# Hybrid attention layer on one core: transfers pinned behind weight pieces, and the query group's parts redistributed

## The chip, the cores and the metric

One NeuronCore of a Trainium2 chip runs the whole kernel. The metric is device time in microseconds (us) of one execution. Engines: PE (TensorE matmul), PEld (its weight load), DVE (VectorE), ACT (ScalarE), POOL (GpSimd) and SP (SyncE, which here only issues transfers).

## The reference

One encoder layer on 1024 tokens of width 2048, all float32:

```
u = rmsnorm(h); z = u @ w_in                    # 2048 x 9216
q, k, v, gate (16 heads x 64), and an HGRN2 group of 8 heads x 128
q = rope(q) / 8;  k = rope(k)
res = [band_attention(q, k, v, w, d) for (w, d) in ((128,1), (512,4), (2048,16))]
o_att = softmax over the three log denominators, weighted sum;  y_att = o_att * silu(gate)
y_hg  = rmsnorm(forward scan + backward scan) * silu(its gate)
h = h + rmsnorm([y_att, y_hg] @ w_out)
h = h + rmsnorm(sigmoid(h @ w_pg) * (p @ w_pp))
```

The change touches the attention heads alone: the products q, k and gate, the banded softmax, and the product with v.

## The kernel before, in words

The stages follow each other: normalise x and project all v (0 to about 400 us), eight HGRN2 heads (to about 1290 us), eight pairs of attention heads (to about 2100 us), then the output projection and the two gates. Every product with a weight matrix is made three times over (high x high, low x high, high x low), so a weight piece of 512 x 128 (256 KB) costs a load on SP, a cast `wh` on ACT (L83), a subtraction `wl` on POOL (L84), a cast `wb` on DVE (L85) and, for both halves of the tokens, 16 matmuls with `wh` and `wl` (L102, L103) and 8 with `wb` (L107). `raw`, `wh`, `wl` and `wb` have three buffers each, so loads run three pieces ahead of PE.

A group (q, k or gate of one pair) is four pieces. `group_parts` is a generator: after the matmuls of a piece that end half 0 of the tokens it yields (16 high and 4 low matmuls: an odd part), and after the 4 low ones of half 1 it yields again (an even part). Eight parts make a group; one more step calls `sink`, which evacuates both halves. A group takes two of the four `gb` banks of PSUM, and there are three kinds of groups in flight, so a group begins when an earlier one's banks have been evacuated. The four other banks (`wk`) serve scores, transposes and values.

`Pair` is a pair of heads:

- `queries()` and `keys()` evacuate through `rope_evac`: `araw` on ACT (L521), an exchange of rows by small transfers into `apart` (L525, L526), `apr` on POOL (L528), `araw` times cosine on DVE (L529), then the sum, `aq` (L576) or `akn` (L557). A key half is then split into `akh` (L560) and `akn` (L561) and copied by four transfers into the key tiles `ak` (L565, L566).
- `q_half(hf)` splits the query half `aq` on ACT (`aqh`, L589) and DVE (L590) and copies it by eight transfers of 128 KB into `aqt` (L594), which has one buffer.
- `loads()` brings V in two arrangements, `avc` (L602, two transfers of 256 KB) and `avn` (L609, four of 64 KB and four of 192 KB), one buffer each.
- `scores(hf, fill)`: eight units of score matmuls `asc` (L637), each reduced and masked on DVE (L646) and exponentiated on ACT (L649), then a softmax exchange: per-query minima and sums are moved between partitions (`aoth`, L657) and turned into factors `afm` (L661 to L670). After every second unit it takes one part from `fill`.
- `values(hf, fill)`: eight turns scale the probabilities (`asm`, L690 on ACT, L692 on DVE), transpose them on PE (`apt`, L694), copy them (`aPT`, L697) and multiply with V (`ao`, L706 with `avn`, L709 with `avc`); then `ayt` (L719). It takes a part of `fill` at the second and the sixth turn.
- `gate()` evacuates with a sigmoid (`sg`, L728), two products (L729, L730) and a store to `yD` (L731).

The evacuations share the tag `h2` with five buffers: `araw`, `apr`, `akn`, `akh`, `aq`, `aqh` and `sg`.

Order: a scheduler orders each engine's instructions ahead of time, by the order in which the program traces them and by when it takes them to be ready; weight pieces (load and casts) are given a priority 3000 places ahead. [...] `keep_in_program_order` fixes an instruction behind the one traced last on its engine, and `after(x, mark)` issues x behind mark; neither adds a wait for a result.

The loop over pairs, before, with a the pair and b the next:

```
a.loads(); g = a.gate(); a.scores(0, g)            # 4 gate parts
run(bq, 4); a.q_half(1); a.values(0, bq); a.scores(1, bq); run(bq)
run(g, 2); run(b.keys(), 9); b.q_half(0); a.values(1, islice(g, 2)); run(g)
```

Of the kernel before, what the change touches and what calls it, by code (L numbers as in the profile page):

```python
# [12 lines left out]
F32 = mybir.dt.float32  # L13
# [9 lines left out]
S = 1024  # L23
# [14 lines left out]
def f32(t):  # L38
    return t.bitcast(F32)
# [6 lines left out]
class Kern:  # L46
    def __init__(self, tc, ctx):
        self.tc = tc
        self.nc = tc.nc
        self.ctx = ctx  # L50
        nc = self.nc
        self.cp = ctx.enter_context(tc.tile_pool(name="cp", bufs=1))
        self.wp = ctx.enter_context(tc.tile_pool(name="wp", bufs=3))
        self.ps = ctx.enter_context(tc.tile_pool(name="ps", bufs=1, space=PSUM))
        self.dr = ctx.enter_context(tc.tile_pool(name="dr", bufs=1, space=DRAM))
        self.ident = self.cp.tile([128, 128], F32, name="ident")
        make_identity(nc, self.ident)
        self.rest = None
# [481 lines left out]
    class Pair:  # L540
        def __init__(self, K, w_in, hp, vsrc, yout):
            self.K, self.w_in, self.hp, self.vsrc, self.yout = K, w_in, hp, vsrc, yout
            self.nat = (slice(0, 64), slice(64, 128))
            self.qn = {}
            self.sm = {}
            self.fac = {}

        def keys(self):
            K, nat = self.K, self.nat
# [32 lines left out]
        def q_half(self, hf):  # L582
            K, nat = self.K, self.nat
            nc = K.nc
            V = nc.vector
            q = self.qn.pop(hf)
            self.QT = [K.big.tile([128, 2, 512], F32R, name=f"aqt{i}", tag=t, bufs=1) for i, t in enumerate(("hv", "O"))]
            qh = K.h2("aqh")
            nc.scalar.copy(qh.bitcast(F32R), q)  # L589
            V.tensor_tensor(q.bitcast(F32R), q, qh, op=ALU.subtract)  # L590
            for sq, src in ((0, qh), (1, q)):
                for h in range(2):
                    for o in range(2):
                        nc.sync.dma_start(f32(self.QT[sq])[nat[o], h], src[nat[h]])  # L594

        def loads(self):
            K, vsrc = self.K, self.vsrc
            nc = K.nc
            self.vn = K.big.tile([128, 8, 2, 128], F32, name="avn", tag="ht", bufs=1)
            self.vc = K.big.tile([128, 4, 2, 128], F32, name="avc", tag="hvt", bufs=1)  # L600
            for k in range(2):
                nc.sync.dma_start(self.vc[:, :, k], vsrc[512 * k:512 * k + 512, :].rearrange("(p r) e -> p r e", r=4))  # L602
            row = vsrc.ap[0][0]
            for i0, st, n in ((0, 7, 2), (1, 1, 6)):
                t0 = K.wstart(i0)
                step = (K.wstart(i0 + st) - t0) * row
                for r in range(4):
                    src = bass.AP(tensor=vsrc.tensor, offset=vsrc.offset + (t0 + r) * row, ap=[[4 * row, 64], [step, n], [1, 128]])
                    nc.sync.dma_start(self.vn[64 * (r % 2):64 * (r % 2) + 64, i0:i0 + st * (n - 1) + 1:st, r // 2], src)  # L609
            self.yt = K.big.tile([128, S], F32, name="ayt", tag="gt", bufs=1)  # L610

        def scores(self, hf, fill):
            K, KS, QT = self.K, self.KS, self.QT
# [57 lines left out]
            self.sm[hf] = sm  # L671
            self.fac[hf] = m

        def values(self, hf, fill):
            K, vn, vc, yt = self.K, self.vn, self.vc, self.yt
            nc = K.nc
            V = nc.vector
            sm, f = self.sm.pop(hf), self.fac.pop(hf)
            o = K.wk("ao")
            ov = o.rearrange("p (i r b) -> p i r b", i=4, r=4)  # L680
            steps = [(l, i) for i in range(4) for l in range(2)]
            pt = {}

            def turn(n):
                l, i = steps[n]
                p = K.wk("apt", (128, 2, 2, 128))
                for h in range(2):
                    d = sm[h][:, l, i]
                    if h:
                        nc.scalar.activation(d, d, AF.Copy, scale=f[:, l, h, i:i + 1])  # L690
                    else:
                        V.tensor_scalar(d, d, f[:, l, h, i:i + 1], None, op0=ALU.mult)  # L692
                    for c in range(2):
                        nc.tensor.transpose(p[:, h, c], d[:, 128 * c:128 * c + 128], K.ident)  # L694
                if n % 2 == 0:
                    pt[n // 2] = K.big.tile([128, 2, 2, 2, 128], F32, name="aPT", tag=("KD", "hq")[n // 2 % 2], bufs=1)
                (nc.scalar.copy if n % 2 else V.tensor_copy)(pt[n // 2][:, n % 2], p)  # L697

            def use(n):
                l, i = steps[n]  # L700
                P = pt[n // 2][:, n % 2]
                for c in range(2):
                    for h in range(2):
                        hs = slice(64 * h, 64 * h + 64)
                        if l:
                            nc.tensor.matmul(o[hs, 128 * i:128 * i + 128], vn[:, 4 * hf + i, c, hs], P[:, h, c],  # L706
                                             start=False, stop=(n == 7 and c == 1), skip_group_check=True)
                        else:
                            nc.tensor.matmul(ov[hs, :, i, :], vc[:, i, c, hs], P[:, h, c].rearrange("p (i b) -> p i b", i=4),  # L709
                                             start=(n == 0 and c == 0), stop=False, skip_group_check=True)  # L710

            for n in range(10):
                if n < 8:
                    turn(n)
                if n in (1, 5):
                    next(fill, None)
                if n >= 2:
                    use(n - 2)
            nc.scalar.copy(yt[:, 512 * hf:512 * hf + 512].rearrange("p (i b r) -> p i r b", i=4, r=4), ov)  # L719

        def gate(self):
            K = self.K
            nc = K.nc

            def sink(hf, p):
                sl = slice(512 * hf, 512 * hf + 512)
                sg = K.h2("sg")
                nc.scalar.activation(sg, p, AF.Sigmoid)  # L728
                nc.vector.tensor_tensor(sg, p, sg, op=ALU.mult)  # L729
                nc.gpsimd.tensor_tensor(sg, sg, self.yt[:, sl], op=ALU.mult)  # L730
                nc.sync.dma_start(self.yout[:, sl], sg)  # L731
            return K.group_parts(self.w_in, 3072 + 128 * self.hp, sink)


# [1 line left out]
def tile_hybrid(ctx, tc, x, p, positions, w_in, w_out, g_pre, g_post, g_hg, lb_fwd, lb_bwd, w_pg, w_pp, g_ple, out):  # L736
    nc = tc.nc
    K = Kern(tc, ctx)
# [52 lines left out]
    with tc.tile_pool(name="big", bufs=1) as big:  # L791
        K.big = big
        for h in range(8):
            K.hgrn(w_in, h, vD[2 + h // 4][:, 128 * (h % 4):128 * (h % 4) + 128], yD[8 + h])
            if h == 0:
                with tc.issue_after(late[0].ins), tc.issue_after(late[1].ins):
                    K.att_consts(positions)
        heads = [K.Pair(K, w_in, hp, vD[hp // 4][:, 128 * (hp % 4):128 * (hp % 4) + 128], yD[hp]) for hp in range(8)]

        def run(parts, n=8):  # L800
            for _ in range(n):
                next(parts, None)

        run(heads[0].queries(), 9)
        K.flush()
        run(heads[0].keys(), 9)
        heads[0].q_half(0)
        for n, a in enumerate(heads):
            b = heads[n + 1] if n < 7 else None
            a.loads()  # L810
            g = a.gate()
            if n == 0:
                run(g, 4)
            a.scores(0, g)
            bq = b.queries() if b else iter(())
            run(bq, 4)
            a.q_half(1)
            a.values(0, bq if b else g)
            a.scores(1, bq if b else islice(g, 1))
            run(bq)  # L820
            if b:
                if n:
                    run(g, 2)
                run(b.keys(), 9)
                b.q_half(0)
            a.values(1, islice(g, 1 if n == 7 else 2) if n else iter(()))
            run(g)
    fin = ctx.enter_context(tc.tile_pool(name="fin", bufs=1))
    Y = [fin.tile([128, 4, D], F32, name=f"Y{i}", tag=f"Y{i}") for i in range(2)]
    yss = [fin.tile([128, 4, 4], F32, name=f"yss{i}") for i in range(2)]  # L830
# [255 lines left out]
```

## Time and profile before

| what | us |
|---|---|
| median of 3 runs | 2906.26 (2904.66 to 2910.24) |
| the profiled execution's own time | 2900.24 |
| its span, first to last instruction | 2898.5 |
| PE busy | 2726.5 (94%) |
| attention stage, 1290 to 2100 us | 810, PE busy 745.07 |
| stops of PE at the changes of pair, 1 to 6, and their ends | 9.54 to 1430.44, 4.22 to 1530.27, 4.88 to 1629.62, 4.44 to 1728.71, 5.05 to 1828.22, 5.59 to 1928.10 |
| stops before the first transpose of `values(0)`, pairs 0 to 6 | 1.82, 2.04, 1.78, 1.79, 1.78, 1.79, 1.78 |

A busy time is that of one engine's instructions. A row of the waits gives the waiting engine, line and tile, what released it, then the total in us, how often, and the longest. A row in order of time gives start, duration, engine, line, operation, output and inputs, how many were merged, and in brackets how long the engine had been idle before it and what ended that. A row for a window gives busy time (and number of instructions) of PE, PEld, DVE, ACT and POOL, then the clock granted to PE (1.00 is full), the share of the 16 DMA engines' time, and GB/s. In the rows below, SPq is SP's queue of transfers to issue.

### The profile page before, as it was taken

What the parts mean: (1) busy time and instruction counts of PE and PEld (TensorE: products, weight loads), DVE (VectorE), ACT (ScalarE), POOL (GpSimd) and SP (SyncE); (2) the same over time, 40 slices, a digit from 0 to 9 for tenths busy, and PEclk for the clock granted to TensorE, in tenths of its full rate; (3) what the DMA queues carried; (4) which work ended last, traced back from release to release, by engine and by line L of the source; (5) the groups of instructions that cost most, each with busy time, mean ns of one, the idle gap of its engine ahead of it and who ended that gap; (6) DMA issues with size and microseconds to landing.
All of it is one profiled execution on the core that took longest, in us unless ns stands there. A gap on an engine that the chain in (4) does not pass through costs nothing. (4 is left out here: it accounts for less than half of the span.)

```text
span 2898.5 us, 45014 instructions
## 1 busy us (share of the span) xinstructions
PE 2726.5 (94%) x16853; PEld 1893.5 (65%) x17104; DVE 1449.1 (50%) x3105; ACT 951.3 (33%) x1998; POOL 1047.7 (36%) x833
## 2 busy tenths in 40 slices
PE   6999999999999999999899999989899899999997
PEld 4666666666676666676666666667566566666664
DVE  8601116856356356354555445544755545555545
ACT  5311112222122122123445445544733233333323
POOL 2422223313313313322222232222244554666555
PEclk9999999999999999999999999999999999999998
DMA  6412221211111111123323332342444543444453
GB/s 226 123 55 78 79 84 41 66 49 41 59 49 41 59 49 41 59 59 89 101 59 90 104 97 55 99 108 78 124 139 133 157 146 95 133 113 111 141 155 112
DMA packets 272218, 267.75 MB, mean 92 GB/s; under 512 B 22784, under 2 KB 187648, under 8 KB 270848
## 3 DMA queue, kind: packets, MB, share of 16 engines
q1 hardware_dynamic: 262832, 255.92, 30.7%
q10 hardware_dynamic: 9168, 8.93, 0.9%
q8 instruction: 135, 2.21, 0.3%
q14 instruction: 83, 0.68, 0.1%
HBM read 208.16 MB, written 29.36 MB: 82 GB/s over the span
## 5 line engine op out<-in xcount | busy, mean ns | idle before, releaser
L84 POOL TENSOR_TENSOR wl<-raw,wh 128x512 fp32r<-128x512 f32 x568 | 771.0, 1361 | 1520.7 <-ACT wh L83 1484.0
L85 DVE CAST wb<-raw 128x512 bf16<-128x512 f32 x584 | 406.6, 699 | 817.2 <-PE gb L107 311.8
L83 ACT CAST wh<-raw 128x512 fp32r<-128x512 f32 x584 | 358.1, 617 | 1280.2 <-PE gb L102 474.7
L102 PE MATMUL gb<-uh,wh 128*128 128x512 f32 x1792 | 743.2, 415 | 24.3 <-DMA aqt<-aqh 19.7
L103 PE MATMUL gb<-uh,wl 128*128 128x512 f32 x1792 | 709.5, 396 | 0.0
L107 PE MATMUL gb<-ul,wb 128*128 128x512 bf16 x1635 | 407.6, 380 | 9.0 <-issue 1.3
L102 PEld LDWEIGHTS gb<-uh,wh 128*128 128x128 f32 x1792 | 339.9, 190 | 110.0 <-DVE sg L729 27.0
L103 PEld LDWEIGHTS gb<-uh,wl 128*128 128x128 f32 x1792 | 339.7, 190 | 67.9
L107 PEld LDWEIGHTS <-wb 128*128 128x128 bf16 x1792 | 156.9, 98 | 205.0 <-issue 53.6
L868 PE MATMUL gb<-wh,yh 128*128 128x512 f32 x512 | 231.5, 453 | 7.5 <-DVE Y L900 3.4
L868 PE MATMUL gb<-wh,th 128*128 128x512 f32 x480 | 215.1, 448 | 0.0
L869 PE MATMUL gb<-wl,yh 128*128 128x512 f32 x512 | 203.5, 398 | 5.5 <-POOL wl L84 5.5
L869 PE MATMUL gb<-wl,th 128*128 128x512 f32 x480 | 189.7, 395 | 5.3 <-POOL wl L84 5.3
L872 PE MATMUL gb<-wb,yl 128*128 128x512 bf16 x481 | 136.0, 386 | 1.4 <-issue 0.2
L649 ACT ACTIVATE asm<-asm,aown 128x256 f32<-128x256 f32 x256 | 127.1, 498 | 23.0 <-DVE aown L646 22.5
L872 PE MATMUL gb<-wb,tl 128*128 128x512 bf16 x452 | 126.2, 385 | 1.0
L868 PEld LDWEIGHTS gb<-wh,yh 128*128 128x128 f32 x512 | 97.9, 191 | 37.9 <-issue 3.4
L767 PE MATMUL gb<-wh,uh 128*128 128x512 f32 x256 | 115.4, 457 | 2.0 <-ACT wh L83 2.0
L869 PEld LDWEIGHTS gb<-wl,yh 128*128 128x128 f32 x512 | 97.7, 191 | 25.7 <-POOL wl L84 6.8
L768 PE MATMUL gb<-wl,uh 128*128 128x512 f32 x256 | 101.5, 403 | 10.1 <-POOL wl L84 7.1
L868 PEld LDWEIGHTS gb<-wh,th 128*128 128x128 f32 x480 | 91.0, 190 | 27.5 <-ACT sg L972 2.0
L869 PEld LDWEIGHTS gb<-wl,th 128*128 128x128 f32 x480 | 90.7, 189 | 25.1 <-POOL wl L84 7.6
(284 smaller groups left out, 3646.6 us busy)
## 6 DMA issues: line engine op xcount, KB each, us to landing
raw<-in_w_in_dram SPq DMA_DIRECT2D x320, 256.0 KB
raw<-in_w_out_dram SPq DMA_DIRECT2D x128, 256.0 KB
raw<-in_w_pg_dram SPq DMA_DIRECT2D x128, 256.0 KB
xt<-in_x_dram SPq DMA_DIRECT2D x8, 1024.0 KB
vD<-vo SPq DMA_DIRECT2D x32, 256.0 KB
aqt<-aqh SPq DMA_DIRECT2D x64, 128.0 KB
aqt<-aq SPq DMA_DIRECT2D x64, 128.0 KB
raw<-yD SPq DMA_DIRECT2D x32, 256.0 KB
```

Of the source, the lines that this page charges most:

```text
L83: nc.scalar.copy(wh, raw)
L84: (sub or nc.gpsimd).tensor_tensor(wl, raw, f32(wh), op=ALU.subtract)
L85: nc.vector.tensor_copy(wb, raw)
L102: nc.tensor.matmul(pb[hf], wh[:, k], self.uh[hf][:, kt], start=(kt == 0), stop=False)
L103: nc.tensor.matmul(pb[hf], wl[:, k], self.uh[hf][:, kt], start=False, stop=False)
L107: mm = nc.tensor.matmul(pb[hf], wb[:, k], self.ul[hf][:, kt], start=False, stop=(kt == KT - 1))
L649: nc.scalar.activation(d, d, AF.Exp, scale=-1.0, bias=own[:, 0, loc, h, i:i + 1], accum_out=own[:, 1, loc, h, i:i + 1])
L767: nc.tensor.matmul(pb[t], hi, wh, start=(k == 0), stop=False)
L768: nc.tensor.matmul(pb[t], hi, wl, start=False, stop=False)
L868: nc.tensor.matmul(pb[t], a, pc[0], start=first, stop=False)
L869: nc.tensor.matmul(pb[t], a, pc[1], start=False, stop=False)
L872: nc.tensor.matmul(pb[t], lo[:, k, 128 * t:128 * t + 128], pc[2], start=False, stop=last)
```

## The change

Three things. (1) The transfers of `q_half`, `loads` and the gate's store, which the scheduler placed freely, are each fixed behind what SP had been given before them in the program. `loads()` moves from ahead of the scores to behind the first scores and their gate pieces, and the store of a pair's gated output moves out of the evacuation to the same place in the next pair, ahead of `loads()`. (2) The fills are dealt out anew: five query parts instead of four come before `values(0)`, whose first transpose is issued behind the fifth; `values(0)` and `scores(1)` take one and two; the query evacuation follows `scores(1)`; the first pair keeps two gate parts for `values(1)`; the last pair spreads its gate group over the places where others have queries. (3) `b.q_half(0)` moves from behind the key group to behind its fifth part, and the first transpose of `values(1)` is issued behind the eighth key part.

```diff
@@ Pair.q_half
-                        nc.sync.dma_start(f32(self.QT[sq])[nat[o], h], src[nat[h]])
+                        K.tc.keep_in_program_order(nc.sync.dma_start(f32(self.QT[sq])[nat[o], h], src[nat[h]]))
@@ Pair.loads: both transfers go through this
+            def load(dst, src):
+                K.tc.keep_in_program_order(nc.sync.dma_start(dst, src))
...
-            self.yt = K.big.tile([128, S], F32, name="ayt", tag="gt", bufs=1)
+        def store(self):
+            for sl, sg in self.out:
+                self.K.tc.keep_in_program_order(self.K.nc.sync.dma_start(self.yout[:, sl], sg))
@@ Pair.values
-        def values(self, hf, fill):
+        def values(self, hf, fill, mark):
...
-                        nc.tensor.transpose(p[:, h, c], d[:, 128 * c:128 * c + 128], K.ident)
+                        x = nc.tensor.transpose(p[:, h, c], d[:, 128 * c:128 * c + 128], K.ident)
+                        if n == h == c == 0 and mark is not None:
+                            K.after(x, mark)
@@ Pair.gate
-                nc.sync.dma_start(self.yout[:, sl], sg)
+                self.out.append((sl, sg))
+            self.yt = K.big.tile([128, S], F32, name="ayt", tag="gt", bufs=1)
@@ the loop over pairs
         def run(parts, n=8):
-            for _ in range(n):
-                next(parts, None)
+            return [next(parts, None) for _ in range(n)]
...
-            a.loads()
             g = a.gate()
             if n == 0:
                 run(g, 4)
-            a.scores(0, g)
-            bq = b.queries() if b else iter(())
-            run(bq, 4)
+            bq = b.queries() if b else g
+            a.scores(0, g if 0 < n < 7 else islice(g, 2))
+            if n:
+                heads[n - 1].store()
+            a.loads()
+            marks = run(bq, 5 if b else 3)
             a.q_half(1)
-            a.values(0, bq if b else g)
-            a.scores(1, bq if b else islice(g, 1))
-            run(bq)
+            a.values(0, islice(bq, 1), marks[-1])
+            a.scores(1, islice(bq, 2 if b else 1))
             if b:
+                run(bq)
                 if n:
                     run(g, 2)
-                run(b.keys(), 9)
+                k = b.keys()
+                run(k, 5)
                 b.q_half(0)
-            a.values(1, islice(g, 1 if n == 7 else 2) if n else iter(()))
+                marks = run(k, 4)
+            a.values(1, islice(g, 2 if b else 0), marks[2] if b else None)
             run(g)
+        a.store()
```

More of the change, by code (lines that the diff above doesn't have):

```diff
@@ L546, in __init__ @@
             self.fac = {}
+            self.out = []
         def keys(self):
@@ L601, in loads @@
             for k in range(2):
-                nc.sync.dma_start(self.vc[:, :, k], vsrc[512 * k:512 * k + 512, :].rearrange("(p r) e -> p r e", r=4))
+                load(self.vc[:, :, k], vsrc[512 * k:512 * k + 512, :].rearrange("(p r) e -> p r e", r=4))
             row = vsrc.ap[0][0]
@@ L608, in loads @@
                     src = bass.AP(tensor=vsrc.tensor, offset=vsrc.offset + (t0 + r) * row, ap=[[4 * row, 64], [step, n], [1, 128]])
-                    nc.sync.dma_start(self.vn[64 * (r % 2):64 * (r % 2) + 64, i0:i0 + st * (n - 1) + 1:st, r // 2], src)
-            self.yt = K.big.tile([128, S], F32, name="ayt", tag="gt", bufs=1)
+                    load(self.vn[64 * (r % 2):64 * (r % 2) + 64, i0:i0 + st * (n - 1) + 1:st, r // 2], src)
+        def store(self):
+            for sl, sg in self.out:
+                self.K.tc.keep_in_program_order(self.K.nc.sync.dma_start(self.yout[:, sl], sg))
         def scores(self, hf, fill):
```

## The prediction

> **What bounds the kernel now.** I read the page's busy shares first, then the waits of PE over the attention stage (1290 to 2100 us), then PE, SP and ACT in order of time around one change of head pair.
>
> ```profile
> span 2898.5 us, 45014 instructions
> PE 2726.5 (94%) x16853; PEld 1893.5 (65%) x17104; DVE 1449.1 (50%) x3105; ACT 951.3 (33%) x1998; POOL 1047.7 (36%) x833
> 1290.00:2100.00 810.00, 745.07 (x4299) 535.70 (x4368) 417.96 (x1364) 395.15 (x1012) 226.90 (x213) 0.97 0.34 90
> PE gb L102 <- DMA aqt<-aqh: 19.7, 4, 5.6
> PE apt L694 <- DVE asm L692: 16.3, 10, 2.2
> PE asc L637 <- DMA aqt<-aqh: 9.5, 1, 9.5
> PE gb L102 <- DVE sg L729: 4.4, 1, 4.4
> PE asc L637 <- DMA aqt<-aq: 3.4, 2, 3.1
> ```
>
> PE is the bound: 94% busy, and in attention 745 of 810 us. The third row is a window (PE, PEld, DVE, ACT, POOL busy, clock, DMA share, GB/s). The rest are PE's stops: total, times, longest. Two kinds matter: one long stop per head pair, where PE waits for the transposed query copies (aqt) or for a gate's PSUM bank (sg): 19.7 + 9.5 + 4.4 = 33.6 us over the six changes of pair; and one short stop per pair before the first probability transpose (apt), 16.3 us in all. Attention rows repeat every 99 us, so one change stands for six.
>
> ```profile
> 1524.15 1.90 PE L107 MATMUL gb<-ul,wb 128*128 128x512 bf16 x8
> 1530.27 0.50 PE L102 MATMUL gb<-uh,wh 128*128 128x512 f32 x1 [4.22 <-DMA aqt<-aqh]
> 1513.90 0.70 SPq L525 DMA_DIRECT2D apart<-araw  x1
> 1516.79 1.26 SPq L602 DMA_DIRECT2D avc<-vD  x2
> 1518.14 3.22 SPq L609 DMA_DIRECT2D avn<-vD  x5
> 1522.95 0.63 SPq L565 DMA_DIRECT2D ak<-akh  x1
> 1525.01 0.61 SPq L566 DMA_DIRECT2D ak<-akn  x1
> 1525.72 0.56 SPq L594 DMA_DIRECT2D aqt<-aqh  x1
> 1528.90 2.52 SPq L594 DMA_DIRECT2D aqt<-aq  x4
> 1531.84 1.42 SPq L731 DMA_DIRECT2D yD<-sg  x2
> 1522.73 0.61 ACT L589 CAST aqh<-aq 128x512 fp32r<-128x512 f32 x1
> 1527.60 1.28 ACT L728 ACT_TABLE_LOAD   x1 [2.86 <-DMA ak<-akh]
> 1524.00:1532.00 8.00, 3.78 (x16) 1.95 (x15) 1.86 (x4) 3.60 (x6) 2.91 (x3) 0.94 0.88 233
> ```
>
> PE runs out at 1526.05 and restarts at 1530.27. SP issues one DMA per 0.6 us: seven V loads, then the keys' last four copies, then the eight query copies, until 1531.4; the DMA engines are 88% busy. Two lags end together: the query copies land near 1530.6, and the gate's sigmoid, which must first get an h2 buffer that a key copy still reads (ACT released at 1527.60), frees the bank the next query group needs.
>
> **The change, part by part.** *Query half 0 moves from behind the keys to behind five of their eight parts.* It issues one ACT cast (0.61 us), one DVE subtraction (0.69, row below), eight DMAs (8 x 0.6 = 5 us of SP). They hang behind the third key piece's weight load. In the trace the second q half is summed at 1588.56 to 1590.7, and SP issues nothing but two weight loads from 1591 to 1599.5, so I put the copies there, 25 us before they are needed, and at nothing on PE. If that cover fails, they push the keys' row exchange, issued next at 1599.48, by up to 5 us, and the keys' copies and scores with it.
>
> ```profile
> 1523.46 0.68 DVE L590 TENSOR_TENSOR aq<-aq,aqh 128x512 fp32r<-128x512 f32 x1
> 1588.56 2.18 DVE L576 TENSOR_TENSOR aq<-araw,apr 128x512 f32<-128x512 f32 x1 [2.40 <-POOL apr L528]
> 1591.05 4.15 SPq L76 DMA_DIRECT2D raw<-in_w_in_dram  x2
> 1599.48 0.64 SPq L525 DMA_DIRECT2D apart<-araw  x1
> ```
>
> Late next: the key copies. They still go out at 1522.95 to 1525.6 and, by ACT's release at 1527.60, land about then. PE would wait 1527.60 - 1526.05 = 1.55 us, unless the next query piece runs first; its bank comes free sooner, since two h2 buffers (aq, aqh) are back before the keys' evacuation and the sigmoid need not wait for the key copies. So each stop goes to between 0 (piece first) and 1.55 (scores first). I take the middle, 0.8, as the order on PE is fixed and I can't see it: 33.6 - 6 x 0.8 = 28.8 us saved. Were the copies no earlier at all, nothing would be.
>
> *The clock.* After a long stop PE runs at half clock. Rows: start of a stop's aftermath for pairs 1, 2, 6 (pairs 3 to 5 read 0.79 too), the aftermath of pair 0's 3.1 us stop, and that of the short stop (last):
>
> ```profile
> 1430.00:1438.00 8.00, 7.47 (x31) 6.24 (x32) 3.78 (x12) 3.19 (x7) 4.06 (x5) 0.66 0.71 190
> 1530.00:1538.00 8.00, 7.73 (x36) 6.38 (x37) 3.87 (x14) 2.77 (x5) 3.87 (x6) 0.79 0.79 215
> 1928.00:1936.00 8.00, 7.83 (x30) 6.29 (x30) 2.31 (x8) 1.76 (x5) 3.64 (x5) 0.64 0.79 214
> 1342.00:1350.00 8.00, 7.95 (x35) 6.46 (x36) 0.99 (x4) 1.40 (x4) 0.74 (x2) 0.79 0.27 75
> 1552.00:1560.00 8.00, 6.77 (x62) 4.91 (x64) 5.24 (x13) 5.58 (x13) 0.89 (x2) 1.00 0.01 2
> ```
>
> Lost work is 8 x (1 - clock): 2.7 + 4 x 1.7 + 2.9 = 12.4 us. A 1.78 us stop leaves 1.00, so with stops of 0.8 all 12.4 us come back. If they stay at 3 us, none does. [...]
>
> *Five parts before the first transpose.* The stop after the softmax exchange:
>
> ```profile
> 1550.80 0.59 PE L107 MATMUL gb<-ul,wb 128*128 128x512 bf16 x2
> 1553.18 1.06 PE L694 MATMUL apt<-ident,asm 128*128 128x128 f32 x8 [1.78 <-DVE asm L692]
> 1536.04 0.42 DVE L646 CUSTOM_DVE_ANT_0 asm<-asc,amask 128x256 f32<-128x256 f32 x1 [2.61 <-PE asc L637]
> ```
>
> The fifth part's 16 high matmuls and two of its low ones already run before the stop; the order edge adds only two low ones (0.23 us each), 0.5 us. Two larger shifts come with it: PE reaches this place 1.7 us sooner without half clock, while the scores start sooner against the query piece: now the first reduction comes 1536.04 - 1530.27 = 5.8 us after it, then about 1527.6 + 1.2 (four score matmuls and a query one or two) - 1526.05 = 2.75, 3.0 us better. 1.78 - 0.5 + 1.7 - 3.0 = 0. Ends: 0 and 1.78 + 1.7. Near 0 in the sum, I keep 0.3 per pair: six stops of 1.78 to 2.04 (sum 11.0) become 2, saved 9.
>
> *Stores and V loads.* Twelve DMAs per pair (1.4 us and 10 x 0.63 us of SP) go behind the scores' gate pieces. They then follow the store, issued at 1531.84 already, to about 1540; at 233 GB/s the V tiles' 1.5 MB (2 x 256, 4 x 192 and 4 x 64 KB) and the store's 0.5 MB take 9 us, landed by 1542. First use is after the transposes at 1553: no wait, 10 us of margin. What waits behind them on SP: weight loads, run three pieces (16 us) ahead, and the second query half's copies, now issued at 1538.67 to 1549.9 and used from 1563. Zero; lower end zero too, upper end whatever exceeds 10 us.
>
> *Fills redistributed.* Pair 0 gains two gate parts (5.4 us) in front of the 9.5 us stop, already counted as removed. The same matmuls run. Query evacuation now follows all of the second scores: keys need its banks.
>
> ```profile
> 1563.02 1.21 PE L637 MATMUL asc<-ak,aqt 128*128 128x256 f32 x8
> 1571.85 0.39 PE L102 MATMUL gb<-uh,wh 128*128 128x512 f32 x1
> 1576.72 0.59 ACT L521 ACTIVATE araw<-gb 128x512 f32<-128x512 f32 x1
> 1577.74 0.58 PE L102 MATMUL gb<-uh,wh 128*128 128x512 f32 x1
> 1579.74 0.51 ACT L649 ACTIVATE asm<-asm,aown 128x256 f32<-128x256 f32 x1 [1.40 <-DVE aown L646]
> 1581.69 0.23 ACT L664 ACTIVATE afe<-afe 128x32 f32<-128x32 f32 x1 [1.35 <-DVE afe L663]
> 1583.08 1.31 ACT L690 ACTIVATE asm<-asm,afm 128x256 f32<-128x256 f32 x3 [1.16 <-DVE afm L670]
> ```
>
> Keys start at 1577.74, right behind the evacuation at 1576.72. Behind the last exponential (ends 1580.3) the two evacuations end at 1581.5, against PE work (scores 4.8, query piece 5.6, gate piece 5.4 from 1563.0) that ends at 1578.8: 2.7 us of stop. But that exponential was itself late because rope work took DVE, so the lower end is 0. I take 1.0: +6 over six pairs. Pair 0 keeps its first stop; its short one gives 1. The last pair, with 2 us of stops and thin fills either way, gives 0.
>
> **Sum.** 28.8 + 12.4 + 9 + 1 - 6 = 45 us off the profiled execution's 2900.24 (span 2898.5 and 1.7 around it): 2855. The median of the runs, 2906.26, lies 6.0 (0.2%) above; carried over, 2861.
>
> **Rivals.** *Half the gain*: PE's fixed order puts the scores ahead of the query piece, and the key copies land later than the order was made for, so stops of about 3 us stay. Saved: 33.6 - 18 = 15.6 of the first kind, no clock (by the 3.11 us row), 5 of the short ones, less 6: 15, 2891. [...] For it: every stop now is such a mismatch of order and landing. Against it: 1.55 us is all that the keys' landing leaves.
>
> *The same bytes, no gain*: the boundary is bound by the transfers (88% busy), and the order does not matter: 2906. Against it: 1 MB of query copies (8 x 128 KB) goes to 1591 to 1600, where the engines have room, and the V loads' 1 MB leaves too. [...]
>
> *Slower*: the query evacuation falls on ACT behind the scaling of the second half's probabilities (1583.08 to 1587) and keys wait for the banks: 1588.2 - 1578.8 = 9.4 us and 1.7 of half clock, 11 a pair, 66 over six instead of 6. 2861 + 60 = 2921. It decides for slower once the stop passes some 7 us with its clock 8.5. For it: ACT's order is fixed and there are only four group banks. Against it: the scaling is traced after the keys, the evacuation before.
>
> **How the numbers follow.** Forecast (2840 to 2880) 0.58; half the gain (2880 to 2900) 0.22; no gain 0.06; slower 0.14. A measurement tells about 0.2%, 6 us, from no change: faster 0.80, same 0.06, slower 0.14. The range leaves out the slower case and a little below: both ends of key landing and exchange give 2861 - 5 - 2 - 6 = 2848 at best and 2861 + 5 + 19 + 10 = 2895 at worst, widened to 2842 and to 2905, so that the half-gain case is in.
>
> **What would show it.** Right: the stops on aqt and sg gone or under 1.6 us, clock 1.00 at the change of pair, query copies 25 us ahead of the scores, period near 92 instead of 99 us. Wrong: a new stop in front of keys released by ACT's evacuation (L521), a wait for avc or avn at L709 or L706, or weight casts released by late DMAs (SP blocked behind a pinned copy).

## The result, and the profile after

| | before | changed |
|---|---|---|
| median of the runs, us | 2908.25 (2904.66 to 2910.72, 4 runs) | 2862.28 (2859.64 to 2864.40, 4 runs) |
| profiled execution, us | 2900.24 | 2864.40 |

Changed over before: 0.9842, 95% interval [0.9825, 0.9859], so 1.6% faster, 46 us by the medians. The two profiled executions differ by 36 us only: that of before lies 8 us under its median, that of the changed kernel 2 us above. The traces are therefore read for the places, and the medians for the size.

The changed kernel's page, and PE's waits between the first scores of pair 1 and those of pair 7, first of before, then of after:

```profile
span 2862.6 us, 45162 instructions
PE 2733.1 (95%) x17104; PEld 1891.4 (66%) x17104; DVE 1433.7 (50%) x3105; ACT 949.0 (33%) x1996; POOL 1045.1 (37%) x833
```

```profile
PE gb L102 <- DMA aqt<-aqh: 19.7, 4, 5.6
PE apt L694 <- DVE asm L692: 11.0, 6, 2.0
PE asc L637 <- DMA aqt<-aqh: 9.5, 1, 9.5
PE gb L102 <- DVE sg L729: 4.4, 1, 4.4
PE asc L637 <- issue: 1.2, 1, 1.2
```

```profile
PE asc L645 <- DMA ak<-akn: 22.8, 7, 4.2
```

Five kinds of stop, 45.8 us, have become one, 22.8 us: the scores wait for the key copies. Six of the seven are those at the changes of pair 1 to 6 (19.9 us); the seventh, 2.90 us before the scores of pair 7, stands where before had the 1.2 us of `issue`. (Line numbers have moved down, for the transfers of queries and keys by 1, for the scores by 8, for the gate by 10.) The waits for query copies, for the gate's banks and for the scaled probabilities are gone. The new stop, its surroundings on PE, SP and ACT, and the clock after it (from the stop's end, pair 2, then pairs 5 and 6):

```profile
1508.75 1.90 PE L107 MATMUL gb<-ul,wb 128*128 128x512 bf16 x8
1514.14 1.04 PE L107 MATMUL gb<-ul,wb 128*128 128x512 bf16 x4
1518.04 0.72 PE L645 MATMUL asc<-ak,aqt 128*128 128x256 f32 x4 [2.86 <-DMA ak<-akn]
1478.50 2.45 SPq L595 DMA_DIRECT2D aqt<-aqh  x4
1483.78 1.22 SPq L595 DMA_DIRECT2D aqt<-aq  x2
1512.83 0.67 SPq L566 DMA_DIRECT2D ak<-akh  x1
1513.61 0.53 SPq L76 DMA_DIRECT2D raw<-in_w_in_dram  x1
1515.59 0.61 SPq L567 DMA_DIRECT2D ak<-akn  x1
1518.54 1.26 SPq L602 DMA_DIRECT2D avc<-vD  x2
1512.83 1.28 ACT L738 ACT_TABLE_LOAD   x1
1518.00:1526.00 8.00, 7.96 (x42) 6.72 (x43) 5.34 (x27) 6.42 (x20) 2.10 (x4) 0.79 0.59 185
1804.00:1812.00 8.00, 7.96 (x48) 6.64 (x48) 6.48 (x35) 7.33 (x23) 1.99 (x3) 1.00 0.76 228
1898.70:1906.70 8.00, 7.92 (x36) 6.79 (x37) 4.02 (x19) 5.21 (x14) 2.12 (x4) 0.61 0.49 149
```

The query copies now go out at 1478.5 to 1485.0, over 30 us ahead of the scores. The gate's sigmoid starts at 1512.83, without the wait for a key copy that it had. The V loads start at 1518.54, behind the keys. But PE does only four of the eight low matmuls of the gate's second piece (L107, the row with x4), then stands before the first score matmul while the last key copy, issued at 1515.59, is under way. The four low matmuls left, and a whole query piece as a run below shows, could have run; the order of PE's instructions was set ahead of time with the scores ahead of them, and PE did them only behind the stop of 2.86 us, two from 1519.31 and two from 1522.31. Five of the six stops leave PE at reduced clock (0.79 over the 8 us behind those of pairs 1 to 4, 0.61 behind pair 6's); one of 3.00 us (ending 1804.05) leaves it at 1.00. From pair to pair it is now 95.1 us instead of 99.

### The profile page after: what moved, and what is told of

Its sections match the earlier page's. It is cut to its first block, busy times and chain, and to the rows that moved or that the text cites. A ratio compares the mean times of both kernels' runs of the same rounds, so it can differ in the third digit from the quotient of the medians.

```text
span 2862.6 us, 45162 instructions
## 1 busy us (share of the span) xinstructions
PE 2733.1 (95%) x17104; PEld 1891.4 (66%) x17104; DVE 1433.7 (50%) x3105; ACT 949.0 (33%) x1996; POOL 1045.1 (37%) x833
## 5 line engine op out<-in xcount | busy, mean ns | idle before, releaser
L107 PE MATMUL gb<-ul,wb 128*128 128x512 bf16 x1792 | 440.0, 383 | 0.0
L107 PEld LDWEIGHTS <-wb 128*128 128x128 bf16 x1792 | 156.6, 98 | 205.3 <-issue 54.8
```

The source lines that it names most:

```text
L107: mm = nc.tensor.matmul(pb[hf], wb[:, k], self.ul[hf][:, kt], start=False, stop=(kt == KT - 1))
```

## The experiments

**One part at a time, on the kernel before.** First the query half alone:

```diff
-                run(b.keys(), 9)
-                b.q_half(0)
+                k = b.keys()
+                run(k, 5)
+                b.q_half(0)
+                run(k, 4)
```

> The kernel before, with only the query half 0 of the next pair moved behind five key parts; its transfers are left unpinned, the V loads stay ahead of the scores, and the fills are the old ones. Theory (the long stop was the query copies and the h2 buffers held behind the keys): the wait on aqt and on sg at the change of pair goes, a wait on the key copies of 1.5 to 2.5 us takes its place, half clock mostly goes; the short stop before apt stays at 1 to 3 us. 2872 to 2885. Rival (the V loads ahead in the queue are what made the copies late): the stops stay at 4 us, 2895 to 2908.

Then the pins and the new places of V loads and stores alone; `q_half`, `loads` and `store` are those of the changed kernel, fills and the place of `q_half(0)` those of before:

```diff
-            a.loads()
             g = a.gate()
...
             a.scores(0, g)
+            if n:
+                heads[n - 1].store()
+            a.loads()
```

> The kernel before, with only the transfers pinned and the V loads and stores moved behind the first scores; the query half stays behind all keys, the fills are the old ones. Theory: the query copies are still issued last and the buffers still held, so the stop only gets shorter by what the V bytes took from the engines, under 1 us a pair: 2896 to 2908. Rival (the queue is the cause): the stops fall under 2 us and the clock stays full, 2865 to 2880.

Then the fills and the two order edges alone: the changed loop and `values`, with transfers, V loads and the query half as before, thus against the changed loop:

```diff
+            a.loads()
             g = a.gate()
...
-            if n:
-                heads[n - 1].store()
-            a.loads()
...
-                run(k, 5)
-                b.q_half(0)
-                marks = run(k, 4)
+                marks = run(k, 9)[5:]
+                b.q_half(0)
```

> The kernel before, with only the fills dealt out anew and the first transposes issued behind the fifth query part and the eighth key part; transfers, V loads and query half as before. Theory: pair 0's 9.5 us stop halves (its gate parts now lie there), the other long stops stay, the short stop loses 0.5 us: 2893 to 2902. Rival (the short stop and the evacuation order are worth as much as the transfers): all short stops go, 2880 to 2888.

| kernel | median, us | over before, 95% interval |
|---|---|---|
| query half alone | 2862.72 | 0.9853 [0.9826, 0.9880] |
| pins and places alone | 2911.69 | 1.0026 [1.0015, 1.0036] |
| fills alone | 2894.76 | 0.9968 [0.9956, 0.9981] |

The kernel before had a median of 2904.19 beside these. The query half alone is worth 41 us, which can't be told from the whole change; the fills are worth 9; the pins and places cost 7.5. The first expectation was too low on the gain, the second missed the sign, the third held in its time, but the short stop lost only 0.2 us of the 0.5 expected (1.78 to 1.57).

Where the pins and places cost is in their trace: the second half's scores now wait for a POOL copy (L636) five times, 0.80 us each, 4.0 us in all, which the kernel before does not, and the clock behind the six long stops is 0.59 to 0.79 instead of 0.64 to 0.79.

With the query half alone (PE's stops in pairs 2 and 5, its last high matmul and the transposes in pair 2, the transfers before the first stop, and the clock behind it):

```profile
1522.85 0.71 PE L637 MATMUL asc<-ak,aqt 128*128 128x256 f32 x4 [1.03 <-DMA ak<-akn]
1806.60 0.72 PE L637 MATMUL asc<-ak,aqt 128*128 128x256 f32 x4 [0.91 <-DMA ak<-akn]
1538.30 0.39 PE L102 MATMUL gb<-uh,wh 128*128 128x512 f32 x1
1540.47 1.06 PE L694 MATMUL apt<-ident,asm 128*128 128x128 f32 x8 [1.78 <-DVE asm L692]
1514.03 3.32 SPq L609 DMA_DIRECT2D avn<-vD  x5
1518.00 0.37 SPq L76 DMA_DIRECT2D raw<-in_w_in_dram  x1
1518.46 0.63 SPq L565 DMA_DIRECT2D ak<-akh  x1
1523.00:1531.00 8.00, 8.00 (x49) 6.41 (x50) 6.25 (x33) 7.62 (x23) 3.84 (x5) 1.00 0.56 166
```

The V loads stand straight ahead of the key copies, as before the change, and still the stop on the keys is only about 1 us in pairs 2 to 6 (pair 1, which has no gate piece left to run there, still waits 5.5 us for its banks), and the clock there stays at 1.00 in four of the five (0.79 in pair 3). So V loads in the queue were not what held PE up. The short stop before the transposes stays: 1.78 us in four of those pairs, 1.99 in the other. The pins alone show it from the other side: with the V loads gone from that place, PE still stops for the query copies, which SP still issues last:

```profile
1530.11 0.77 PE L645 MATMUL asc<-ak,aqt 128*128 128x256 f32 x2 [4.40 <-DMA aqt<-aqh]
1525.31 0.62 SPq L567 DMA_DIRECT2D ak<-akn  x1
1526.03 1.20 SPq L595 DMA_DIRECT2D aqt<-aqh  x2
1529.13 2.52 SPq L595 DMA_DIRECT2D aqt<-aq  x4
1528.29 1.28 ACT L738 ACT_TABLE_LOAD   x1 [3.89 <-DMA ak<-akh]
```

**Is the stop that is left one of PE's order?** The changed kernel, with a query part ahead of the scores:

```diff
-            a.scores(0, g if 0 < n < 7 else islice(g, 2))
+            pre = []
+            if 0 < n < 7:
+                run(g, 4)
+                pre = run(bq, 1)
+            a.scores(0, islice(g, 0 if pre else 2), pre[0] if pre else None)   # first score matmul behind pre[0]
...
-            marks = run(bq, 5 if b else 3)
+            marks = run(bq, 5 - len(pre) if b else 3)
```

> The changed kernel, with the first score matmul of pairs 1 to 6 issued behind the first part of the next pair's query group (20 matmuls, 4.6 us) and behind all of the gate's second piece. Theory (the 3 us left at the change of pair are PE's order: scores put ahead of work that could run while the key copies land): the stop on ak goes, clock 1.00 there, some 1 to 2.5 us return before apt since less work is left over the softmax exchange: 2840 to 2855. Rival (the pair is bound by the chain keys, scores, exchange, values, whatever PE does meanwhile): the stop only moves to apt, 2858 to 2866.

2850.90 us, 0.9812 [0.9791, 0.9832] of before; the interval overlaps a little with that of the changed kernel, the times themselves do not. Pairs 1 to 6 have no stop on `ak` at all; pair 7, left as it was, keeps its own. 1.4 us come back before the transposes. These are the rows of its waits and of that stop:

```profile
PE asc L645 <- DMA ak<-akn: 2.5, 1, 2.5
1535.02 1.06 PE L704 MATMUL apt<-ident,asm 128*128 128x128 f32 x8 [1.39 <-DVE asm L702]
```

**What the pins and places cost beside the rest.** Query half and fills without any pin, V loads and stores in their old places (against the kernel with the fills alone):

```diff
-                marks = run(k, 9)[5:]
-                b.q_half(0)
+                run(k, 5)
+                b.q_half(0)
+                marks = run(k, 4)
```

> The query half moved and the fills dealt out anew, nothing else: no transfer pinned, V loads ahead of the scores and stores in the evacuation as before. Theory (parts add; the pins cost): the key copies' stop is 1 us instead of 3 as with the query half alone, clock 1.00, short stop as in the changed kernel (none): 2848 to 2856, faster than the changed kernel by 0.2 to 0.5%. Rival (pins are worth something once the query half is early): 2862 to 2872.

And the changed kernel with only the V loads put back ahead of the scores and unpinned:

```diff
-                K.tc.keep_in_program_order(nc.sync.dma_start(dst, src))
+                nc.sync.dma_start(dst, src)
...
+            a.loads()
             g = a.gate()
...
-            a.loads()
             marks = run(bq, 5 if b else 3)
```

> The changed kernel with one thing undone: V loads ahead of the scores and unpinned again; query copies and stores stay pinned. Theory (the V loads' new place lets the schedule set the scores five matmuls earlier, ahead of the landing): the stop on ak falls from 3 to 1 us and the time to 2848 to 2856. Rival (the pins themselves cost): unchanged, 2858 to 2866.

Without any pin: 2842.98 us, 0.9794 [0.9778, 0.9810]. With the V loads alone put back: 2846.13, 0.9804 [0.9789, 0.9818]. Both are faster than the 2848 to 2856 expected, and both intervals lie below that of the changed kernel. So the new place of the V loads, with its pin (the run undoes the two together), loses 16 us by the medians, 11 by the ratios to before; the pins on query copies and stores make no difference that these runs can tell. The fills are worth more in this company than alone: the kernel without pins is the query half and the fills, and lies 17 (by the ratios) to 20 us under the query half alone. PE's waits, SP and PE at the same place, the transposes that follow, and the clock, in the kernel without pins:

```profile
PE asc L637 <- DMA ak<-akn: 6.4, 7, 1.3
1510.91 0.37 SPq L76 DMA_DIRECT2D raw<-in_w_in_dram  x1
1511.38 0.63 SPq L565 DMA_DIRECT2D ak<-akh  x1
1513.43 0.61 SPq L566 DMA_DIRECT2D ak<-akn  x1
1512.61 1.90 PE L107 MATMUL gb<-ul,wb 128*128 128x512 bf16 x8
1515.32 0.72 PE L637 MATMUL asc<-ak,aqt 128*128 128x256 f32 x4 [0.59 <-DMA ak<-akn]
1534.21 0.81 PE L107 MATMUL gb<-ul,wb 128*128 128x512 bf16 x3
1534.85 1.04 PE L694 MATMUL apt<-ident,asm 128*128 128x128 f32 x8
1515.00:1523.00 8.00, 7.34 (x44) 6.19 (x46) 7.00 (x33) 6.75 (x20) 4.13 (x5) 1.00 0.53 157
```

All eight low matmuls (x8) now stand ahead of the scores, against four in the changed kernel: 0.9 us. (With the V loads alone put back it is the same: eight from 1512.17, a stop of 0.61 us to 1514.92.) And the keys land sooner against the same PE work: from the start of those low matmuls to the scores it is 2.7 us here, 3.9 in the changed kernel. There SP issued a weight load (1513.61) after the first key copy; here the weight load went out ahead of all four. Of these 1.2 us about half is the later issue of the last key copy (1.45 us behind the start of the low matmuls instead of 0.82), the rest its longer way from issue to the scores (2.45 us instead of 1.89). Together that is the 2 us between the two stops of pair 2. Pair 1 of the changed kernel is another case: there the weight load is ahead of all four copies, and the stop is 3.19 us all the same, since the first key copy goes out 0.16 us behind the start of the low matmuls (1418.82 against 1418.66) and not 1.2 us ahead. Behind pair 2's long stop the clock is 0.79 over 8 us, behind its short one 1.00.

**The four matmuls alone.** The changed kernel with the first score matmul behind all of the gate's second piece:

```diff
-            a.scores(0, g if 0 < n < 7 else islice(g, 2))
+            pre = run(g, 4) if 0 < n < 7 else []
+            a.scores(0, islice(g, 0 if pre else 2), pre[3] if pre else None)   # first score matmul behind pre[3]
```

> The changed kernel with the first score matmul of pairs 1 to 6 issued behind all eight low matmuls of the gate's second piece, which it was set ahead of by four; V loads and pins as changed. Theory (2.1 us more stop than with V loads in front: 0.9 from the four matmuls, 1.2 from key copies that land later because a weight load is issued in their midst): the stop on ak falls from 3.1 to about 2.1 us, and as 2 us of stop leave the clock full, the time falls by 6 x (0.9 + 1.5) = 14: 2845 to 2853. Rival (landing alone): the stop stays at 3 us, 2858 to 2866.

2863.38 us, 0.9848 [0.9826, 0.9870]: no gain that can be told. The stops were shorter, 0.79 to 3.12 us instead of 2.86 to 4.20 (13.4 us instead of 19.9 over pairs 1 to 6), but four of the six still cost the clock (0.79 over the 8 us behind them). Pairs 2 and 4 with their clock, then PE and SP of pair 1, then of pair 2:

```profile
1521.28 1.00 PE L645 MATMUL asc<-ak,aqt 128*128 128x256 f32 x4 [2.11 <-issue]
1521.00:1529.00 8.00, 7.72 (x40) 7.09 (x41) 5.74 (x30) 5.51 (x16) 2.42 (x4) 0.79 0.68 206
1710.68 0.72 PE L645 MATMUL asc<-ak,aqt 128*128 128x256 f32 x4 [2.11 <-issue]
1710.00:1718.00 8.00, 7.10 (x43) 6.25 (x44) 6.25 (x33) 6.21 (x19) 2.80 (x4) 1.00 0.64 191
1424.24 1.90 PE L107 MATMUL gb<-ul,wb 128*128 128x512 bf16 x8
1426.93 0.71 PE L645 MATMUL asc<-ak,aqt 128*128 128x256 f32 x4 [0.79 <-DMA ak<-akn]
1422.31 0.38 SPq L76 DMA_DIRECT2D raw<-in_w_in_dram  x1
1422.79 0.67 SPq L566 DMA_DIRECT2D ak<-akh  x1
1517.27 1.90 PE L107 MATMUL gb<-ul,wb 128*128 128x512 bf16 x8
1515.97 0.67 SPq L566 DMA_DIRECT2D ak<-akh  x1
1516.74 0.53 SPq L76 DMA_DIRECT2D raw<-in_w_in_dram  x1
```

Two stops of the same 2.11 us: behind one the clock is 0.79, behind the other 1.00. The expectation's premise, that 2 us leave the clock full, was wrong. The part of PE's order in the loss is therefore argued from the rows above and from the run with the query part ahead, not shown by this run. For the weight load among the key copies it has a comparison inside one trace: in pair 1 the weight load went out ahead of all four copies, and the scores follow the start of the eight low matmuls by 2.69 us, as without pins; in pair 2 the first key copy is issued 1.30 us ahead of those matmuls (1.45 in pair 1), but the weight load stands behind it, and it is 4.01 us. No run moves the weight load alone.

**Is there more to be had?** Seven query parts ahead of the transposes, in the kernel with the query part ahead of the scores:

```diff
-            marks = run(bq, 5 - len(pre) if b else 3)
+            marks = run(bq, 7 - len(pre) if 0 < n < 7 else 5 if b else 3)
...
-            a.scores(1, islice(bq, 2 if b else 1))
+            a.scores(1, islice(bq, 0 if 0 < n < 7 else 2 if b else 1))
```

> The changed kernel with the first score matmul behind the first query part, as in the run before, and seven query parts instead of five ahead of the first transpose. Theory (PE order is all that is left): the 1.4 us before apt goes too, PE has no stop over 0.7 us in pairs 1 to 6: 2838 to 2846, unless the second scores, which lose 24 matmuls of cover, stop PE by 1 to 2 us before keys or inside the scores. Rival (the softmax chain bounds the pair): 2848 to 2856.

The query part ahead of the scores (the edit shown above) in the kernel without pins:

> Query half moved, fills dealt out anew, first score matmul behind the first query part; no transfer pinned, V loads ahead of the scores. With the scores held back by 4.6 us of query work the landing of the keys no longer counts, so the V loads' place should not matter: within 0.2% of the same kernel with the pins (2851): 2846 to 2856. Rival (V loads ahead make the copies land later than 5 us after PE's arrival): stops on ak of 1 us and more, 2858 and up.

And that with six query parts ahead of the transposes:

```diff
-            marks = run(bq, 5 - len(pre) if b else 3)
+            marks = run(bq, 6 - len(pre) if b else 3)
...
-            a.values(0, islice(bq, 1), marks[-1])
+            a.values(0, islice(bq, 0 if b else 1), marks[-1])
```

> Query half moved, fills dealt out anew, no transfer pinned, first score matmul behind the first query part, and six query parts instead of five ahead of the first transpose. Theory: the 1.38 us stop before apt falls to 0.5 us, six times 0.9 = 5 us off: 2838 to 2844. Rival (the softmax chain follows the extra matmuls): 2843 to 2848.

2846.88 (0.9808 [0.9793, 0.9823]), 2845.17 (0.9802 [0.9788, 0.9817]) and 2847.25 us (0.9795 [0.9777, 0.9814]). None can be told from the 2842.98 us of query half and fills without pins; the first and the third miss the gain that was expected of them. The stops move about: with seven parts the second scores wait 1.2 us per pair for a POOL copy (L636), with six the transposes still wait 0.96 us and the first product with V, in three of the pairs, 0.4 to 0.7. With a query part ahead of the scores, the V loads' place matters little (2850.90 with pins, 2845.17 without, a shade under the range expected).

## Why the prediction was right, and where it was not

The forecast was 2861 us against 2862.28. Its parts were off in both directions, and of its own signs of being right only some came: the stops on query copies and gate banks went and the copies went out early, but the stops that stayed are over 1.6 us, the clock behind five of the six is not 1.00, and the period is 95.1 us, not near 92. (The kernel without pins has 92.1.)

- *Query half moved: right, and alone it gives what the whole change gives.* The copies left over 30 us ahead of the scores, the bank and buffer wait went, and alone the step gives 41 us.
- *"I take the middle, 0.8, as the order on PE is fixed and I can't see it": the step that failed.* The stops that stayed are 3.19, 2.86, 3.48, 3.18, 3.00 and 4.20 us, beyond the stated end of 1.55. The bound took the order before as it stood: PE at the scores at 1526.05, behind all eight low matmuls, and the keys landed at 1527.60, 3.45 us behind the start of those. In pair 2 the scores were set four matmuls (0.86 us) earlier, and the keys landed 3.90 us behind the same start, 0.45 later: 1.55 + 0.86 + 0.45 = 2.86. Saved: 33.6 - 19.9 = 13.7 us, not 28.8. This is the rival *half the gain* at its place.
- *"All 12.4 us come back" (the clock): wrong with it.* 8 x (1 - clock), an estimate of the lost work, after the six stops is now 4 x 1.7 + 0 + 3.1 = 9.9 us, so 2.5 came back. Half clock itself stands in the trace of before: in the three microseconds from 1531, behind pair 2's 4.22 us stop, the clock was 0.51, 0.50 and 0.50, and float32 matmuls of 128x512 that follow each other started 0.43 us apart, from 1535.03 on 0.23.
- *The short stop: right in size, not in its terms.* 11.0 us became 0 in pairs 1 to 6 (the sum had 2). But with the earlier scores and no edge (query half alone) it is still 1.78 us, where the terms for those would leave 0.5: in that order PE does only five high matmuls of the fifth part before the transposes (the last from 1538.30). With the fills and their edge it does all 16 and three low ones (to 1534.85, no stop). So the edge was worth 14 matmuls, some 3 us at 0.23 us each, not two and 0.5; that the fifth part runs ahead anyway held for the order before only.
- *Banks ahead of keys, -6: not there.* No stop of PE lies before the keys; the evacuation of the query group did not hold PE up.
- *V loads and stores at nothing: wrong.* The two terms named, V landing in time and SP's queue, held; what was overlooked is that a transfer's new place changes the order of other instructions too, here of the scores on PE and a weight load on SP. With the pin it cost 11 to 16 us; how that splits between the two is argued above, not shown.
- *Pair 0*: the 9.54 us stop behind it became 3.19, by the two gate parts (5.16 with the fills alone) and the query half (5.49 with that alone); its short stop, put at 1, went from 1.82 to 0.65. *The last pair*, put at nothing, gave about 2 us from its first scores to the end (869.5 to 867.5 us), though some 17 matmuls that ran ahead of them before (562 weight loads on PE in the period up to them, against 544 to 546 in the others) now run behind (4 us at 0.23 us each).

In the profiled executions the sum is 13.7 + 2.5 + 11.0 and some 9 us of smaller items, 36 us. Of the 9, the matmuls moved behind the last pair's scores are 4, the last pair 2 and pair 0's short stop 1.2; pair 7's longer stop takes 1.7 off, and about 3 us are not accounted for. The forecast's 45 and the medians' 46 agree by luck: of the forecast's two largest terms, 41 us, the trace gives 16, and what fills the gap is the short stops, the smaller items and the 10 us by which the medians lie further apart than the profiled executions. Why the kernel before varies more between runs than a trace explains (2899.03 to 2911.07 over 19 runs) stays open.

## What to carry to other kernels

Look for the producer that is issued last though it could be made early: moving one cast, one subtraction and eight copies ahead of other evacuations took away a wait for a transfer, for a buffer and for a PSUM bank at once. When an ahead-of-time scheduler orders the engines, moving a transfer can move other engines' instructions too: read the new order of the engine that bounds the kernel, and keep work that needs no late input behind each wait as a fixed edge. Try each part alone and undo each by itself before keeping the bundle; here the query half alone gave as much as the whole change, the fills were worth 9 us alone and 17 to 20 beside it, and the V loads' new place with its pin took 11 to 16 back.

## What the runs showed of the hardware

In these traces the length of a PE stop did not decide alone whether the clock dropped (read over the 8 us behind it): 2.11 us gave 0.79 once and 1.00 once, in the changed kernel 2.86 us gave 0.79 and 3.00 us 1.00, in the kernel before 3.11 us gave 0.79 and the short stops of pairs 1 to 6, 1.78 to 2.04 us, all left it at 1.00, and of two stops close together (query half alone) 0.75 and 1.16 us in pair 3 gave 0.79, 0.83 and 1.33 us in pair 6 gave 1.00. And taking 1 MB of V loads away from ahead of the key copies brought the scores 0.1 us nearer to the last copy's issue in pair 1 and put them 0.6 us further from it in pair 2: in pair 2, 2.45 us from the issue of the last one to the scores without them (1515.59 to 1518.04, with a weight load among the copies), 1.9 with them (1513.43 to 1515.32); in pair 1, where the weight load went out ahead of the copies in both kernels, 2.16 without and 2.27 with them.
